# One region of program order for ScalarE over both borders of the output projection; first tiles split one per product and loaded three ahead; the last mixed tile taken from SBUF instead of a reload

## The chip, the core and the metric

The kernel runs on one core of one Trainium2 chip. The metric is the device time of one execution, in microseconds (us); smaller is better. The engines work side by side, each through its own queue in order: TensorE (PE) multiplies matrices into PSUM, VectorE (DVE), ScalarE (ACT) and GpSimd (POOL) do elementwise work, and SyncE (SP) here only issues DMA transfers.

## What is computed

Two residual layers on a sequence of 1024 tokens and 1024 channels, fp32 in and out.

```python
def short_conv_mixer(h, w_in, w_conv, w_out):
    proj = h @ w_in                                   # (1024, 4 * 2048)
    b_gate, c_gate, u, z = jnp.split(proj, 4, axis=-1)
    v = c_gate * u
    vp = jnp.pad(v, ((0, 0), (CONV_K - 1, 0), (0, 0)))
    conv = sum(w_conv[k] * vp[:, k:k + S] for k in range(CONV_K))
    return (b_gate * conv * jax.nn.silu(z)) @ w_out

def reference(x, ...):
    x = x + short_conv_mixer(rms_norm(x, conv_norm[0]), conv_w_in[0], conv_w[0], conv_w_out[0])
    x = x + dilated_attention_mixer(rms_norm(x, attn_norm[0]), attn_w_in[0], ...)
    return x
```

The attention layer projects to three groups of queries, keys and values with 16 heads each and to a gate z, does windowed attention in each group, merges the groups and projects back. The change lies in the first layer and in the step from the first to the second.

## The kernel before, in words

**Operands.** Each fp32 operand of a product is held as two parts: a high part in the TensorE's fp32r type, made by a copy on ScalarE, and a low part, the rest, made by a subtraction on VectorE. A product takes three matmuls for each of four k tiles: high by high, high by low, low by high, so 12 matmuls of 128x512 (`product`, L302 to L310). Weights are loaded by SyncE into `wr` (two buffers) and split into `ws` (eight buffers) by `split_w`: ScalarE at L159, VectorE at L160. The activations stand in blocks `blka` to `blkg` and `xb`, each of four tiles with a high and a low part.

**Strassen.** Most of the projections go in pairs of weights by one level of Strassen's scheme: seven products instead of eight, with mixed weights (POOL at L280 into `sr`, three buffers) and mixed activations (T[1] to T[4]). `strassen` (L321) runs the seven products in the order 1, 2, 4 of the pair before, 6, 5, 3 of the pair before, 7, and pulls the next weight split out of the generator `prepare` after each. p1's result is copied out of its PSUM bank by ScalarE (`copied`, L314), then p6 accumulates into the same bank, then comes another copy, then p7 and p4 accumulate in the same way; so each needs the copy before it.

**Stages.** (1) The opening, 0 to about 79 us: the first channel tile e=0 and half of e=1 by plain products (`products`, `first_products`, `evac`), while x is normalised, its row statistics are taken (`row_stats`, `row_spread`) and the mixed activations are made (`mixed`). (2) NI = 29 input pairs, to about 635 us. The results y go to DRAM (`ydc`), and their mixed tiles are made in `y_mix` and stored too (`ymd`). (3) The output projection, to about 810 us: n = NI by plain products a to h, n = NI + 1 to NI + 3 by Strassen, then `chunk` for the second half of the k range, with `row` finishing x1, storing it, and making the attention's operands from it. (4) The attention's projections in pairs, to about 1595 us, then (5) the attention.

**The two borders.** At the first border, from input pairs to the output projection, the blocks change their contents from x to y: `plan` (L469) puts a load of each tile (L474) and its split (L479, L480) into numbered slots, one slot to each product, counted from the first product of n = NI - 1; the load stands two slots ahead of the split. At the second border, from the output projection to the attention's pairs, `row` (L709), `third`, `fourth` and `lower` (L744 to L759) fill the blocks from x1. `fourth` and `lower` load x1 again from DRAM (`x1_tile`, L698).

**What sets the order.** TensorE runs in program order inside a `manual_schedule`. ScalarE does so inside three regions: the opening, n = NI - 1 to NI + 3 (one region for each n), and the stage of `chunk` with the first two pairs of the attention. Everything else, and all of VectorE, POOL and SyncE before the attention, is put in order by a scheduler that simulates the kernel's timeline, and it may move an instruction from outside a region ahead of it.

## Time and profile before

| | |
|---|---|
| Median of three runs | 1926.6 us (1923.59 to 1931.82) |
| The profiled execution | 1925.76 us; its span is 1923.9 us |
| TensorE matmul, weight loads | 1883.5 us busy (98%), 1542.7 us (80%) |
| VectorE, ScalarE, POOL | 1510.4 us (79%), 881.0 us (46%), 950.5 us (49%) |
| DMA | 264.29 MB moved, mean 137 GB/s |
| Busy time of TensorE in 660 to 812 us | 152.00 of 152.00 us |
| Busy time of TensorE in 846 to 1595 us | 747.92 of 749.00 us |
| Busy time of TensorE in 1595 to 1924 us | 307.38 of 329.00 us, granted clock 0.96 |

The profile is one execution, so its stages are set against its own span. Busy time is the time in which an engine had an instruction in work. A matmul of 128x512 shows as 0.39 us, since its end overlaps the next; two in a row start 0.227 us apart at full clock. In a timeline row the first two numbers are the start and the length, and the bracket behind it tells how long the engine had stood idle and what it waited for.

### The profile page before, as it was taken

To read this page: it belongs to the slowest core of one execution; us is meant where nothing else is said; L and a number is where in the kernel's file an instruction comes from. 1 tells how busy PE (TensorE), PEld (TensorE's weight loads), DVE (VectorE), ACT (ScalarE), POOL (GpSimd) and SP (SyncE) were. 2 spreads that over 40 slices of the span, in tenths; PEclk is the share of its full clock that TensorE was granted. 3 is DMA by queue.
4 is the path that set the end of the run, shared out by engine and by line. 5 is a ranking of instruction groups with operands and counts; after the bars stand their busy time and mean duration, and the time that the engine had idled before them with its cause. 6 is when DMAs were issued, how large, how long until landed. Compare 5 with 4: busy or idle time off the path is not lost. (4 is left out here: it accounts for less than half of the span.)

```text
span 1923.9 us, 30568 instructions
## 1 busy us (share of the span) xinstructions
PE 1883.5 (98%) x10814; PEld 1542.7 (80%) x10814; DVE 1510.4 (79%) x2794; ACT 881.0 (46%) x2039; POOL 950.5 (49%) x894
## 2 busy tenths in 40 slices
PE   8999999999999999999999999999999998999999
PEld 6888888888888788878888888888888886777877
DVE  7966667777766865678988698888888887988886
ACT  6533333333334443443334343434343437878880
POOL 1376676767576442524545554555454552333240
PEclk9999999999999999999999999999999999899999
DMA  6222233332423774323324332433232337897742
GB/s 213 87 81 90 89 110 126 109 121 98 127 93 127 236 250 165 136 77 121 115 83 131 109 113 81 136 109 113 83 123 95 125 127 253 248 301 242 223 139 88
DMA packets 121514, 264.29 MB, mean 137 GB/s; under 512 B 19134, under 2 KB 24478, under 8 KB 121360
## 3 DMA queue, kind: packets, MB, share of 16 engines
q1 hardware_dynamic: 94432, 178.99, 28.9%
q0 software_dynamic: 26928, 83.34, 13.0%
q8 instruction: 85, 1.39, 0.3%
q14 instruction: 69, 0.57, 0.1%
HBM read 194.62 MB, written 76.03 MB: 141 GB/s over the span
## 5 line engine op out<-in xcount | busy, mean ns | idle before, releaser
L280 POOL TENSOR_TENSOR sr<-wr 128x512 f32<-128x512 f32 x144 | 207.6, 1442 | 253.3 <-DMA wr<-in_conv_w_in 113.3
L159 ACT ACTIVATE ws<-sr 128x512 fp32r<-128x512 f32 x288 | 180.3, 629 | 325.6 <-PE pp L309 257.4
L160 DVE TENSOR_TENSOR ws<-sr,ws 128x512 fp32r<-128x512 f32 x288 | 269.4, 942 | 66.3 <-ACT ws L159 64.5
L160 DVE TENSOR_TENSOR ws<-wr,ws 128x512 fp32r<-128x512 f32 x248 | 267.2, 1080 | 63.2 <-ACT ws L159 62.7
L159 ACT ACTIVATE ws<-wr 128x512 fp32r<-128x512 f32 x248 | 154.7, 629 | 288.6 <-PE pp L309 242.9
L318 DVE TENSOR_TENSOR f<-pp,f 128x512 f32<-128x512 f32 x216 | 147.3, 682 | 65.0 <-PE pp L309 57.0
L1085 ACT ACTIVATE xs<-xs,nl 128x256 f32<-128x256 f32 (+2 forms) x384 | 160.7, 427 | 0.0
L314 ACT ACTIVATE f<-pp 128x512 f32<-128x512 f32 x240 | 139.3, 581 | 9.5 <-PE pp L309 9.5
L280 POOL TENSOR_TENSOR sr<-wr,sr 128x512 f32<-128x512 f32 x72 | 95.4, 1324 | 77.9 <-issue 67.4
L306 PE MATMUL pp<-blka,ws 128*128 128x512 f32 x328 | 127.8, 390 | 3.0 <-ACT blka L690 2.3
L308 PE MATMUL pp<-blka,ws 128*128 128x512 f32 x328 | 128.0, 390 | 1.4 <-DVE blka L691 1.4
L306 PE MATMUL pp<-blkb,ws 128*128 128x512 f32 x328 | 128.2, 391 | 0.0
L309 PE MATMUL pp<-blka,ws 128*128 128x512 f32 x328 | 127.8, 390 | 0.0
L309 PE MATMUL pp<-blkb,ws 128*128 128x512 f32 x328 | 127.7, 389 | 0.0
L308 PE MATMUL pp<-blkb,ws 128*128 128x512 f32 x328 | 127.6, 389 | 0.0
L306 PE MATMUL pp<-blkg,ws 128*128 128x512 f32 x320 | 124.7, 390 | 0.0
L309 PE MATMUL pp<-blkg,ws 128*128 128x512 f32 x320 | 124.5, 389 | 0.0
L308 PE MATMUL pp<-blkg,ws 128*128 128x512 f32 x320 | 124.5, 389 | 0.0
L306 PE MATMUL pp<-blkf,ws 128*128 128x512 f32 x296 | 118.1, 399 | 3.2 <-ACT f L314 2.9
L1079 DVE CUSTOM_DVE_ANT_0 xs<-ps,bt 128x256 f32<-128x256 f32 (+2 forms) x384 | 102.5, 325 | 21.3 <-PE pt L1092 13.2
L308 PE MATMUL pp<-blkf,ws 128*128 128x512 f32 x296 | 116.1, 392 | 1.0 <-DVE blkf L480 0.7
L309 PE MATMUL pp<-blkf,ws 128*128 128x512 f32 x296 | 115.9, 392 | 0.0
(321 smaller groups left out, 5022.3 us busy)
## 6 DMA issues: line engine op xcount, KB each, us to landing
wr<-in_conv_w_in SPq DMA_DIRECT2D x128, 256.0 KB, 3.1
wr<-in_wqk SPq DMA_DIRECT2D x96, 256.0 KB, 3.2
qkd<-blkc POOLq DMA_DIRECT2D x48, 512.0 KB, 4.3
qk<-qkd SPq DMA_DIRECT2D x48, 512.0 KB, 5.1
f<-in_x SPq DMA_DIRECT2D x48, 256.0 KB, 5.0
f<-ydc SPq DMA_DIRECT2D x48, 256.0 KB, 4.8
wr<-in_wv SPq DMA_DIRECT2D x48, 256.0 KB, 3.1
vd<-blkc POOLq DMA_DIRECT2D x96, 128.0 KB, 2.8
```

What stands on the lines that cost most here:

```text
L159: nc.scalar.activation(t[:, 0], src, AF.Copy)
L160: nc.vector.tensor_tensor(t[:, 1], src, t[:, 0].bitcast(F32), op=OP.subtract)
L280: nc.gpsimd.tensor_tensor(t, x, y, op=op)
L306: nc.tensor.matmul(ps, w[:, 0, ws], b[:, k, 0], start=new and k == 0, stop=False, skip_group_check=skip)
L308: nc.tensor.matmul(ps, w[:, 0, ws], b[:, k, 1], start=False, stop=False, skip_group_check=skip)
L309: nc.tensor.matmul(ps, w[:, 1, ws], b[:, k, 0], start=False, stop=end and k == 3, skip_group_check=skip)
L314: nc.scalar.activation(t, ps, AF.Copy)
L318: nc.vector.tensor_tensor(m, ps, m, op=OP.add)
L1079: nc.vector.tensor_tensor_reduce(out=x, in0=flat[s][:, cols], in1=u["bt"][s][:, bs], op0=OP.add, op1=OP.min, scale=-1.0, scalar=3e38, accu ...
L1085: nc.scalar.activation(x, x, AF.Exp, bias=nm, scale=-1.0, accum_out=L)
```

## The change

The part of the kernel between the two borders becomes one region of program order for ScalarE (`ordered`), entered at n = NI - 1 of the input pairs and left after the first product of pair n = 2 of the attention. TensorE's region begins at the start of the opening instead of behind it, in one piece. The tiles of y are split at most one per product at first, in a new order of blocks (c behind f), and loaded three slots ahead. In n = NI the plain products b and c are exchanged. The first weights of the attention's pairs are split between the last rows (`first_w`, `begun`) instead of ahead of the pairs. The last mixed tile, `fourth(3)`, takes x1 while it is in SBUF in `row(0, 7)`.

```diff
@@ opening of the pools
-            tc.tile_pool(name="pp", bufs=3, space=PSUM) as pp, ... tc.tile_pool(name="cst", bufs=1, space=PSUM) as cst:
+            tc.tile_pool(name="pp", bufs=3, space=PSUM) as pp, ... tc.tile_pool(name="cst", bufs=1, space=PSUM) as cst, \
+            tc.manual_schedule(engines={mybir.EngineType.PE}):
...
-        def strassen(sources, pair, between, made, after=lambda: iter(()), strict=()):
-            w = [list(prepare(*sources[0]))[-1]]
+        def strassen(sources, pair, between, made, after=lambda: iter(()), strict=None, begun=None):
+            w = [begun or list(prepare(*sources[0]))[-1]]
...
-                with tc.manual_schedule(engines={mybir.EngineType.Activation}) if n in strict else nullcontext():
-                    for at, (name, who) in enumerate(order):
+                if n == strict:
+                    ordered.__enter__()
+                for at, (name, who) in enumerate(order):
...
+        ordered = tc.manual_schedule(engines={mybir.EngineType.Activation})
...
-        with tc.tile_pool(name="rp", bufs=1, side="right") as rp, tc.tile_pool(name="cp", bufs=2, side="right") as cp, \
-                tc.manual_schedule(engines={mybir.EngineType.PE}):
+        with tc.tile_pool(name="rp", bufs=1, side="right") as rp, tc.tile_pool(name="cp", bufs=2, side="right") as cp:
...
-                jobs.setdefault(slots[k - 2], []).append(load)
+                jobs.setdefault(slots[min(k - 3, len(slots) - 1)], []).append(load)
...
-            for i, k in enumerate((1, 1, 2, 2)):
-                plan(k, YB, (0, 0), "a", i, ydc[0, i])
-            for i, k in enumerate((3, 3, 4, 4)):
-                plan(k, YB, (1, 0), "b", i, ydc[0, i + 4])
...
-            for i, k in enumerate((7, 7, 8, 8)):
-                plan(k, YT, 1, "c", i, ymd[1, i])
...
+            for ks, d, key, slot in (((1, 2, 3, 4), YB, (0, 0), "a"), ((5, 5, 6, 7), YB, (1, 0), "b"),
+                                     ((6, 7, 8, 8), YB, (1, 1), "d"), ((9, 9, 10, 10), YB, (0, 1), "f"),
+                                     ((11, 11, 12, 12), YT, 1, "c"), ((13, 13, 14, 14), YT, 2, "g"),
...
-                        (0, 0, 0), (0, 0, 1), (1, 0, 0), (1, 0, 1), (0, 1, 0), (1, 1, 0), (0, 1, 1), (1, 1, 1)))}
+                        (0, 0, 0), (1, 0, 0), (0, 0, 1), (1, 0, 1), (0, 1, 0), (1, 1, 0), (0, 1, 1), (1, 1, 1)))}
...
@@ row(hf, dt)
                     if dt < 4:
                         kept[i] = x1
+                    elif dt == 7:
+                        nc.vector.scalar_tensor_tensor(V1[3], x1, g2[:, dt:dt + 1], V1[3], op0=OP.mult, op1=OP.subtract)
@@ fourth(i)
-                t, kt = x1_tile(0, i + 4), i + 4
-                nc.vector.scalar_tensor_tensor(t, t, g2[:, kt:kt + 1], V1[i], op0=OP.mult, op1=OP.subtract)
+                t, kt = V1[3] if i == 3 else x1_tile(0, i + 4), i + 4
+                if i < 3:
+                    nc.vector.scalar_tensor_tensor(t, t, g2[:, kt:kt + 1], V1[i], op0=OP.mult, op1=OP.subtract)
                 parts_of(T[4], i, t)
...
+            first_w = prepare(*sources(pairs[0]))
...
+                    if i == 3:
+                        for _ in range(1 if (hf, dt) == (0, 7) else 2):
+                            w0 = next(first_w)
...
             def between(n, at):
+                if (n, at) == (2, 0):
+                    ordered.__exit__(None, None, None)
...
-            last = strassen([sources(p) for p in pairs], pair, between, lambda: None, strict=range(2))
+            last = strassen([sources(p) for p in pairs], pair, between, lambda: None, begun=w0)
```

Three places show how the instructions move. Line numbers of the changed kernel differ by one or two up to L372 (L159 is L160 there, L314 is L315, L370 is L372) and by more behind that (L479 is L481, L690 and L693 are L678 and L681, L698 is L686, L713 is L701).

**ScalarE in the opening.** Before, ahead of the copy of R (the inverse row norm, out of PSUM bank `st`), behind the last squares of x: `ws` from one `wr` tile are the two halves of one weight tile; in turn W(0, 3), W(1, 0), W(1, 1) and the weights 1 and 2 of the first Strassen pair.

```order
L159 ACTIVATE ws_381<-wr_378 128x512
L159 ACTIVATE ws_384<-wr_378 128x512
L159 ACTIVATE ws_576<-wr_573 128x512
L159 ACTIVATE ws_579<-wr_573 128x512
L159 ACTIVATE ws_677<-wr_674 128x512
L159 ACTIVATE ws_680<-wr_674 128x512
L159 ACTIVATE ws_770<-wr_764 128x512
L159 ACTIVATE ws_773<-wr_764 128x512
L241 ACTIVATE R_125<-st_437 128x512
L242 ACTIVATE sqacc_83<-R_125 128x512
```

Of the changed kernel, the same engine from the second copy of R on: only `ws_383` and `ws_386` stand ahead of the first copy now, and W(1, 0) stands here, behind SiLU and the two taps of tile e=0.

```order
L242 ACTIVATE R_127<-st_521 128x512
L243 ACTIVATE sqacc_83<-R_127 128x512
L365 ACTIVATE f_531<-f_531 128x512
L372 ACTIVATE g_535<-vb_467,conv_w_68 128x512
L372 ACTIVATE g_567<-vb_467,conv_w_68 128x512
L160 ACTIVATE ws_578<-wr_575 128x512
L160 ACTIVATE ws_581<-wr_575 128x512
```

Further on in the changed kernel, from the taps of e=1 to the copy of p1 of the first Strassen pair: all six weights that are split from the pair's loads and mixes and the last mixed tile of x stand between them.

```order
L372 ACTIVATE g<-vb,conv_w 128x512 x2
L160 ACTIVATE ws<-wr 128x512 x2
L160 ACTIVATE ws<-sr 128x512 x3
L160 ACTIVATE ws<-wr 128x512
L160 ACTIVATE ws<-sr 128x512
L206 ACTIVATE blkf<-f 128x512 x4
L315 ACTIVATE f<-pp 128x512
```

The eight splits have gone from one run ahead of R to their places in the program, each close to the product that uses it.

**ScalarE at the first border.** Before, from the second half of b to p7's copy (L314) of the last input pair: `blkc` is a mixed tile out of `ymd`.

```order
L479 ACTIVATE blkb<-f 128x512 x2
L479 ACTIVATE blkc<-f 128x512 x2
L159 ACTIVATE ws<-wr 128x512
L370 ACTIVATE g<-vb,conv_w 128x512
L479 ACTIVATE blkd<-f 128x512 x2
L314 ACTIVATE f<-pp 128x512
L479 ACTIVATE blkd<-f 128x512 x2
```

The same place in the changed kernel:

```order
L481 ACTIVATE blka<-f 128x512
L372 ACTIVATE g<-vb,conv_w 128x512
L481 ACTIVATE blkb<-f 128x512 x2
L315 ACTIVATE f<-pp 128x512
L481 ACTIVATE blkb<-f 128x512
L481 ACTIVATE blkd<-f 128x512
L481 ACTIVATE blkb<-f 128x512
L481 ACTIVATE blkd<-f 128x512
```

The splits of c and d have moved behind the copy, and c behind f.

**SyncE at the second border.** Before, the loads of x1 for `row` (L713), for `fourth` and `lower` (L698), and the weights of the first three attention pairs:

```order
L713 DMA f<-x1d 128x512 x4
L154 DMA wr<-in_wqk 128x512 x4
L713 DMA f<-x1d 128x512 x3
L154 DMA wr<-in_wqk 128x512 x4
L713 DMA f<-x1d 128x512 x2
L698 DMA f<-x1d 128x512 x3
L154 DMA wr<-in_wv 128x512 x3
L698 DMA f<-x1d 128x512 x2
L154 DMA wr<-in_wv 128x512
L698 DMA f<-x1d 128x512 x3
```

And in the changed kernel:

```order
L701 DMA f<-x1d 128x512 x4
L155 DMA wr<-in_wqk 128x512 x4
L701 DMA f<-x1d 128x512 x4
L155 DMA wr<-in_wqk 128x512
L701 DMA f<-x1d 128x512
L155 DMA wr<-in_wqk 128x512 x3
L686 DMA f<-x1d 128x512 x3
L155 DMA wr<-in_wv 128x512 x4
L686 DMA f<-x1d 128x512 x4
```

The load of row (1, 7), and then that of row (0, 7), have moved ahead of the second pair's weights; one reload of `fourth` is gone, and all four of `lower` stand behind the four weight loads of the third pair, where the first stood ahead of the fourth of them.

## The prediction

> **What bounds the kernel now.** I read the page first, then the busy time stage by stage, then the waits of TensorE, then the timelines of the engines around each of its gaps.

> ```profile
> span 1923.9 us, 30568 instructions
> PE 1883.5 (98%) x10814; PEld 1542.7 (80%) x10814; DVE 1510.4 (79%) x2794; ACT 881.0 (46%) x2039; POOL 950.5 (49%) x894
> ```

> TensorE works for 98% of the span, and its 1925.76 us run is the span and 1.86 us around it. Nothing in the change removes a matmul. So it can only give back time in which TensorE stood or ran slowly, or add such time. Columns of the next view: stretch, its length, then busy time of each engine; behind POOL stand the granted clock of TensorE, the DMA share and GB/s.

> ```profile
> 0.00:80.00 80.00, 71.96 (x316) 58.71 (x317) 66.06 (x113) 48.24 (x79) 15.59 (x22) 1.00 0.54 180
> 80.00:635.00 555.00, 553.16 (x2428) 453.95 (x2426) 396.97 (x434) 209.20 (x362) 366.38 (x301) 1.00 0.33 107
> 635.00:643.00 8.00, 5.11 (x16) 3.85 (x15) 8.00 (x9) 5.17 (x10) 5.05 (x3) 0.79 0.50 167
> 654.00:660.00 6.00, 5.27 (x22) 3.75 (x21) 6.00 (x7) 3.56 (x7) 4.71 (x6) 1.00 0.54 169
> 812.00:818.00 6.00, 5.42 (x23) 3.95 (x22) 4.44 (x7) 2.77 (x5) 3.10 (x3) 1.00 0.35 125
> 834.00:846.00 12.00, 8.25 (x27) 6.27 (x27) 10.14 (x13) 6.04 (x11) 5.02 (x3) 0.72 0.25 82
> ```

> The first border (635 to 643, and an echo at 654) and the second (812 to 846) lose time, and at 0.79 and 0.72 the clock was down too. The 555 us of input pairs lose only 1.8 us: nothing of size is to be had there, but much can be lost. The waits of TensorE between 400 and 900 us name who was late (total, times, longest):

> ```profile
> PE pp L306 <- ACT f L314: 4.7, 3, 2.9
> PE pp L306 <- ACT blka L690: 2.3, 1, 2.3
> PE pp L308 <- DVE blka L691: 1.4, 1, 1.4
> PE pp L308 <- DVE blkf L480: 0.7, 1, 0.7
> ```

> **Border 1, what goes.** The timelines of TensorE, of ScalarE and of POOL:

> ```profile
> 634.85 0.39 PE L309 MATMUL pp<-blka,ws 128*128 128x512 f32 x1
> 638.13 0.50 PE L306 MATMUL pp<-blkf,ws 128*128 128x512 f32 x1 [2.89 <-ACT f L314]
> ...
> 642.83 0.39 PE L308 MATMUL pp<-blkb,ws 128*128 128x512 f32 x1
> ```

> ```profile
> 632.70 0.63 ACT L479 ACTIVATE blkc<-f 128x512 fp32r<-128x512 f32 x1 [3.74 <-DMA f<-ymd]
> 633.85 0.63 ACT L479 ACTIVATE blkc<-f 128x512 fp32r<-128x512 f32 x1 [0.51 <-DMA f<-ymd]
> ...
> 635.84 0.72 ACT L370 ACTIVATE g<-vb,conv_w 128x512 f32<-128x512 f32 x1 [0.84 <-DVE vb L639]
> ...
> 637.51 0.57 ACT L314 ACTIVATE f<-pp 128x512 f32<-128x512 f32 x1
> ```

> ```profile
> 632.08 1.29 POOL L638 TENSOR_TENSOR f<-f,sqacc 128x512 f32<-128x512 f32 x1 [8.57 <-DVE f L318]
> ```

> Matmuls start 0.227 us apart elsewhere (553.16 us for 2428 of them in the input pairs is 0.228 each). The last of tile `a` starts at 634.85, so the next was due at 635.08; it came at 638.13, 3.05 late. It is p4 of the last input pair, and accumulates into the bank that p7's copy (L314) has to read first; ScalarE waited for two DMAs of the mixed tile c (the split hoisted out of the next region), which also kept VectorE from making `vb`. From 638.13 to 642.83 thirteen steps took 4.70 instead of 2.95: 1.75 more, at about half the clock. Together **4.8 us**. In the new order the splits of c come four products later, and ahead of p7's copy stand only splits whose ydc tiles are loaded long before. What is late next is the chain c12 (VectorE), its product with R2 (POOL), `vb`, taps, two b splits, copy: from the end of the last p3 that is 0.68 + 1.29 + 0.68 + 0.72 + 1.1 + 0.57 and handovers, some 5.3 us, against the 5.4 us of the product and the tile in between. A remaining wait of 0 to 1 us, I take 0.3: **−4.5**. The echo at 654 to 660 is a wait for VectorE's L480; f is now split ahead of c and loaded three products ahead: of some 1.3 us lost (6.00 less 5.27, and restarts at 0.33 for 0.23) I take **−1.0** (0 to −1.3).

> **Border 2.** TensorE, ScalarE and the DMA issues of SyncE's queue:

> ```profile
> 836.48 0.50 PE L306 MATMUL pp<-blka,ws 128*128 128x512 f32 x1 [2.30 <-ACT blka L690]
> 838.43 0.80 PE L308 MATMUL pp<-blka,ws 128*128 128x512 f32 x1 [1.45 <-DVE blka L691]
> ...
> 844.40 0.39 PE L308 MATMUL pp<-xb,ws 128*128 128x512 f32 x1
> ```

> ```profile
> 835.18 0.72 ACT L693 ACTIVATE blkb<-f,attn_norm 128x512 fp32r<-128x512 f32 x1 [4.16 <-DMA f<-x1d]
> 835.81 0.61 ACT L690 ACTIVATE blka<-f 128x512 fp32r<-128x512 f32 x1
> ```

> ```profile
> 827.92 1.63 SPq L154 DMA_DIRECT2D wr<-in_wv  x3
> 829.65 0.84 SPq L698 DMA_DIRECT2D f<-x1d  x2
> ```

> The last mixed tile (`fourth(3)`) needs x1 reloaded from DRAM, and that load stands behind three weight loads: issued at 829.65, split at 835.81. Counting steps as above, the two waits cost 2.46 + 1.72 and the slow matmuls to 844.40 about 2.5: **6.7 us**. The change makes that tile in `row(0, 7)` while x1 is still in SBUF: one VectorE operation is moved, a 256 KB DMA falls, so this wait is gone. Its cost in the new place is one L711 (0.75, as L753 today) ahead of blkf's low part, on a VectorE that the 812 to 818 row shows busy for 4.44 of 6 us; there today's waits (6.00 less 5.42, and two restarts, 1.2 us) end because the loads of rows (1, 7) and (0, 7) now stand ahead of the second wqk tile; I take 0.2 left: **−1.0**. What is late next: the four reloads of `lower` now stand behind all four wv loads instead of one of them ahead of the fourth, and their VectorE low parts have `spread`'s transpose (which frees the bank `st`) queued behind them. By today's row a reload issued at 829.65 was split at 835.18; four of them at about 0.7 each end near 839 to 840, and p3 of the first attention pair, two products behind p4, wants them at about 839. So **+2.0** (0, if they land as the first does today, to 4, as the 2.30 and 1.45 above with a fall of the clock). Sum of border 2: −6.7 − 1.0 + 2.0 = **−5.7**; both borders: **−11.2** (−7.5 to −13.5).

> **The opening, where I see the price.** The order of ScalarE moves here too, although no line of the opening changed: the eight weight splits that ran ahead of R are now two, and the others stand at their place in the program.

> ```profile
> 31.75 2.18 ACT L159 ACTIVATE ws<-wr 128x512 fp32r<-128x512 f32 x4
> 37.19 1.28 ACT L159 ACTIVATE ws<-wr 128x512 fp32r<-128x512 f32 x2 [3.26 <-PE pp L391]
> 40.11 0.63 ACT L159 ACTIVATE ws<-wr 128x512 fp32r<-128x512 f32 x1 [1.65 <-DMA wr<-in_conv_w_in]
> 42.60 0.63 ACT L159 ACTIVATE ws<-wr 128x512 fp32r<-128x512 f32 x1 [1.85 <-PE pp L391]
> ...
> 57.72 0.63 ACT L159 ACTIVATE ws<-sr 128x512 fp32r<-128x512 f32 x1
> ```

> ```profile
> 46.53 1.21 DVE L65 TENSOR_TENSOR rtt<-rt 128x4 f32<-128x4 f32 x1
> 59.96 0.68 DVE L160 TENSOR_TENSOR ws<-sr,ws 128x512 fp32r<-128x512 f32 x1
> 76.79 0.67 DVE L412 TENSOR_TENSOR vb<-pp,f 128x512 f32<-128x512 f32 x1
> 77.53 0.71 ACT L370 ACTIVATE g<-vb,conv_w 128x512 f32<-128x512 f32 x1
> ```

> ```profile
> 57.52 0.39 PE L389 MATMUL pp<-blka,ws 128*128 128x512 f32 x1
> 79.28 0.39 PE L306 MATMUL pp<-blka,ws 128*128 128x512 f32 x1
> PE st L240 <- DVE rt L67: 1.2, 1, 1.2
> ```

> First a gain: POOL's weight mixes no longer stretch the small VectorE operations of the second row statistic (1.21 at 46.53 us), so TensorE's 1.2 us wait for rt goes: −1.2. Then four waits:
> - W(1, 0), today at 57.52 without a wait. Its splits now follow the taps, in the place of the one at 57.72, so the high half comes at 58.35 and the low half, whose place on VectorE is that at 59.96, at 60.6. The third matmul, due 0.45 after the first, waits some 2.7; with the 1.2 gained the chain itself starts earlier as well: +2.4.
> - W(1, 1): its low halves stand behind L410 of the product that has only just ended: L410, a low part of blke, ws, three times 0.68, less 0.45: +1.7.
> - p1 of the first pair, at 79.28 today: splits behind the second taps, which wait for `vb` of the product that just ended: 0.67 + 0.71 + 0.63 and two handovers to the high half, 0.3 more to the low one: +2.5.
> - p6 of that pair: p1's copy now stands behind six splits, one of which needs a POOL mix whose buffer comes free late, and four of blkf. Eleven operations at 0.545 (x4 in 2.18) are 6.0 us against the 5.4 of two products; with the mix (some 1.3, as POOL's row at 632.08) and handovers: +2.2.

> Sum −1.2 + 8.8 = **+7.6**. The lower end is 3, if the queues ahead run dry earlier than my replay says; the upper 15, if they bring down the clock as at 638.13. Does an idle TensorE slow there? 2.89 us of waiting did it, 2.30 and 1.45 close together did it, while this one, without a slow matmul behind it, did not:

> ```profile
> 1596.64 3.43 PE L1064 MATMUL ps<-qk 64*64 64x128 f32 x48 [2.04 <-DVE ps L994]
> ```

> My four waits lie at and above 2.04 and below 2.89, each some 11 us from the next but the last two; I leave the clock out of the sum and put it among the rivals, at 3 in 10. [...]

> **Input pairs, and the rest.** In the pairs with z, SiLU now comes ahead of the taps and of a split, and it waits for POOL's product with R; the copy that p7's bank waits for stands behind it. The first row of the waits has 4.7 − 2.9 = 1.8 us in two such places today. I count four new ones of 0.6 to 1.1 and two old ones gone (1.3): **+1.5** (−1.3 to 3.5). The spread-out splits of a, and loads three ahead, cost nothing while TensorE runs through these pairs (553.16 of 555 us); without that cover a split is 0.63. The swap of (0, 0, 1) and (1, 0, 0) only gives blkb one product, 2.7 us, more. The attention is in the same order on every engine.

> **Sum.** −11.2 + 7.6 + 1.5 = −2.1 on 1925.76, that is 1923.7; the median of the three runs, 1926.6, lies 0.84 above the profiled one, so I say **1924.5**: no change that can be told, since a measurement of this kernel tells about 0.5%, 9.6 us, from no change.

> **Rivals.**
> - The opening hides its splits (a net of −1 to +1): for it, VectorE and ScalarE together have free time there (66.06 and 48.24 of 80 us). Against it, three of the four splits wait for a product that has just ended, which no free time mends. Then 1926.6 − 11.2 and about +1: 1916. Chance 0.18.
> - Slower: the clock falls in the opening. Each fall costs 1.75 (638.13) to 2.5 us (838.43), and a slow spell at each of the four waits is about +8.5: 1933; with the upper ends of the waits 1937. It decides from the point where the opening takes more than the 11.2 less 1.5 that the rest brings. For it: 2.30 and 1.45 us together sufficed. Against: 2.04 did not. Chance 0.17.
> - The border change doesn't do what it says: p7's copy stays late since c12 goes through POOL and VectorE just ahead of it. If 3 us remain at border 1 and 4 at border 2, −11.2 becomes −5.5: about 1930. Chance 0.10.
> - The forecast: 0.55, by itself 1919 to 1930.

> Range 1914 to 1935: it takes in the hidden opening and the third rival, and leaves out the upper end of the slow clock. Faster by over 0.5% (below 1917) 0.18; slower by over 0.5% (above 1936.2) 0.10; within it 0.72.

> **What would show it.** Right: no wait of p4 for the copy near 638 and none for blka near 836, a clock of 1.00 in both stretches, and 635 to 846 shorter by 9 to 13 us; in 0 to 100 us a TensorE busy share that is lower, with waits for ws and vb at W(1, 0), W(1, 1), p1 and for the copy at p6. Wrong: an opening no longer than now, slow matmuls at 0.43 us between 55 and 95 us, or a new wait for blkb or for `st` at about 840 us of over 4 us.

## The result, and the profile after

The changed kernel takes 1943.55 us (median of six runs, 1937.88 to 1945.26) against 1928.32 us for the kernel before (six runs, 1923.59 to 1934.17). The ratio is 1.0078 with a 95% interval of 1.0060 to 1.0095: slower by 0.8%, some 15 us. The prediction said 1924.5 in a range of 1914 to 1935, and gave slower by over 0.5% a chance of 0.10. It was wrong.

The profiled run of the changed kernel took 1945.26 us, its span 1943.5, so 19.6 us more than the profiled span before. The account below is made between these two traces. That it is 19.6 here and 15 between medians comes from the place of the two profiled runs: 1925.76 lies below five of the six runs of before, and 1945.26 is the highest of its six.

TensorE executes almost the same matmuls in the same order in both, so the clearest account is the start of the same matmul in both traces, and how the difference grows:

| matmul | before | after | difference | grown by | forecast for this step |
|---|---|---|---|---|---|
| p1 of the first pair | 79.28 | 86.56 | +7.3 | | |
| p5 of the first pair | 87.44 | 99.92 | +12.5 | +12.5 | +7.6 |
| p7 of the input pair at 553 us | 553.45 | 572.89 | +19.4 | +7.0 | +1.5 |
| last p3 of the input pairs | 645.35 | 660.22 | +14.9 | −4.6 | −4.5 |
| product on blkd behind the blkf products | 660.25 | 680.24 | +20.0 | +5.1 | −1.0 |
| p6 (xb) of the first attention pair | 816.42 | 835.30 | +18.9 | −1.1 | −1.0 |
| first transposes of rtok in `spread` | 848.04 | 867.95 | +19.9 | +1.0 | −4.7 |
| end of the span | 1923.9 | 1943.5 | +19.6 | −0.3 | 0 |

The waits of TensorE in the changed kernel, in 0 to 100 us, 100 to 635 us, and 635 to 900 us (total, times, longest). Line numbers are those of the changed kernel. In the first stretch TensorE also waited 6.7 us for the very first weights (6.1 before) and 0.7 us for R (0.8 before):

```profile
PE pp L307 <- ACT f L315: 2.8, 1, 2.8
PE pp L393 <- DVE ws L161: 2.2, 2, 1.2
PE pp L307 <- ACT ws L160: 2.1, 1, 2.1
PE pp L391 <- ACT ws L160: 1.3, 2, 0.7
```

```profile
PE pp L307 <- ACT f L315: 6.0, 9, 1.4
```

```profile
PE st L104 <- DVE f L110: 4.8, 1, 4.8
PE pp L309 <- DVE blkf L482: 1.6, 2, 0.9
PE pp L307 <- ACT blkf L481: 1.2, 1, 1.2
```

The first four are the opening's four waits that the prediction named, in the places it named. The next is the input pairs: nine waits of p7 for the copy, where the kernel before had two with 1.8 us. In the last three the long waits of before are gone (the copy at the first border, blka at the second), and two others stand there: blkf at 671 us and the bank st at 862 us. TensorE's timeline at three of these places (start, length, and in the bracket the wait):

```profile
57.13 0.50 PE L391 MATMUL pp<-blka,ws 128*128 128x512 f32 x1 [0.62 <-ACT ws L160]
57.46 0.40 PE L392 MATMUL pp<-blka,ws 128*128 128x512 f32 x1
58.87 0.78 PE L393 MATMUL pp<-blka,ws 128*128 128x512 f32 x1 [1.01 <-DVE ws L161]
59.45 0.63 PE L391 MATMUL pp<-blka,ws 128*128 128x512 f32 x1
```

```profile
671.08 0.50 PE L307 MATMUL pp<-blkf,ws 128*128 128x512 f32 x1 [1.18 <-ACT blkf L481]
672.46 0.50 PE L309 MATMUL pp<-blkf,ws 128*128 128x512 f32 x1 [0.88 <-DVE blkf L482]
...
674.16 0.80 PE L309 MATMUL pp<-blkf,ws 128*128 128x512 f32 x1 [0.74 <-DVE blkf L482]
674.75 0.63 PE L310 MATMUL pp<-blkf,ws 128*128 128x512 f32 x1
```

```profile
861.96 1.12 PE L104 MATMUL st<-ident,ms 128*128 128x128 f32 x4 [4.79 <-DVE f L110]
862.73 0.78 PE L307 MATMUL pp<-blkd,ws 128*128 128x512 f32 x1
863.30 0.63 PE L309 MATMUL pp<-blkd,ws 128*128 128x512 f32 x1
```

A length of 0.63 instead of 0.39 us is a matmul at half clock: the granted clock there is 0.50. Behind each of these three places, and behind p6's wait at 95.47 us, matmuls then start 0.427 us apart, at a granted clock of 0.50 for 3.41 us (from 58.92 and 96.47 us) or 6.83 us (from 673.32 and 861.06 us); that adds 1.7 to 2.9 us each time.

What TensorE waits for at 671 us is seen on ScalarE:

```profile
659.68 0.62 ACT L160 ACTIVATE ws<-sr 128x512 fp32r<-128x512 f32 x1
669.87 0.63 ACT L365 ACTIVATE f<-f 128x512 f32<-128x512 f32 x1 [9.57 <-POOL f L631]
670.41 1.14 ACT L481 ACTIVATE blkf<-f 128x512 fp32r<-128x512 f32 x2
```

The second half of blkf's splits stands behind the last SiLU (L365), which waits 9.57 us for POOL's product of c12 with R. At 862 us it is a load. SyncE's queue, then ScalarE:

```profile
848.00 2.11 SPq L155 DMA_DIRECT2D wr<-in_wv  x4
850.15 10.24 SPq L686 DMA_DIRECT2D f<-x1d  x4
```

```profile
855.44 0.72 ACT L681 ACTIVATE blkb<-f,attn_norm 128x512 fp32r<-128x512 f32 x1 [3.30 <-DMA f<-x1d]
```

The four reloads of `lower` go out behind all four weight loads of the third pair; ScalarE and then VectorE wait for the first of them, and the transpose that frees st (L110) stands on VectorE behind its low part and four more operations, from 856.20 to 861.20 us.

### The profile page after: what moved, and what is told of

Its sections match the earlier page's. It is cut to its first block, busy times and chain, and to the rows that moved or that the text cites. A ratio compares the mean times of both kernels' runs of the same rounds, so it can differ in the third digit from the quotient of the medians.

```text
span 1943.5 us, 30568 instructions
## 1 busy us (share of the span) xinstructions
PE 1888.3 (97%) x10814; PEld 1542.3 (79%) x10814; DVE 1483.0 (76%) x2794; ACT 873.7 (45%) x2039; POOL 938.6 (48%) x894
## 3 DMA queue, kind: packets, MB, share of 16 engines
q8 instruction: 85, 1.39, 0.3%
## 5 line engine op out<-in xcount | busy, mean ns | idle before, releaser
L161 DVE TENSOR_TENSOR ws<-wr,ws 128x512 fp32r<-128x512 f32 x248 | 262.4, 1061 | 94.0 <-ACT ws L160 93.7
L161 DVE TENSOR_TENSOR ws<-sr,ws 128x512 fp32r<-128x512 f32 x288 | 264.6, 924 | 81.3 <-ACT ws L160 80.1
L160 ACT ACTIVATE ws<-sr 128x512 fp32r<-128x512 f32 x288 | 179.2, 628 | 326.0 <-PE pp L310 239.6
L160 ACT ACTIVATE ws<-wr 128x512 fp32r<-128x512 f32 x248 | 154.0, 626 | 220.5 <-PE pp L310 197.8
L315 ACT ACTIVATE f<-pp 128x512 f32<-128x512 f32 x240 | 139.4, 581 | 9.0 <-PE pp L310 9.0
L309 PE MATMUL pp<-blka,ws 128*128 128x512 f32 x328 | 127.6, 389 | 0.0
L309 PE MATMUL pp<-blkb,ws 128*128 128x512 f32 x328 | 127.6, 389 | 0.0
L309 PE MATMUL pp<-blkg,ws 128*128 128x512 f32 x320 | 124.5, 389 | 0.0
L307 PE MATMUL pp<-blkf,ws 128*128 128x512 f32 x296 | 118.9, 402 | 1.2 <-ACT blkf L481 1.2
L307 PE MATMUL pp<-blke,ws 128*128 128x512 f32 x288 | 113.4, 394 | 6.2 <-ACT f L315 6.0
L309 PE MATMUL pp<-blkf,ws 128*128 128x512 f32 x296 | 116.7, 394 | 1.6 <-DVE blkf L482 1.6
```

The costliest lines, as they stand in the source:

```text
L160: nc.scalar.activation(t[:, 0], src, AF.Copy)
L161: nc.vector.tensor_tensor(t[:, 1], src, t[:, 0].bitcast(F32), op=OP.subtract)
L307: nc.tensor.matmul(ps, w[:, 0, ws], b[:, k, 0], start=new and k == 0, stop=False, skip_group_check=skip)
L309: nc.tensor.matmul(ps, w[:, 0, ws], b[:, k, 1], start=False, stop=False, skip_group_check=skip)
L315: nc.scalar.activation(t, ps, AF.Copy)
```

## The experiments

The theory to test (R): the region does not begin at n = NI - 1 but where its object is made. `ordered = tc.manual_schedule(...)` stands ahead of the opening, and only `__enter__` stands at n = NI - 1. ScalarE's order in the opening and in every input pair is then the program's, not the scheduler's, and the first 19.4 us of the table are the price. The rival (T) was that the loads three ahead and the new table of splits make the waits of the pairs. For the two borders, the question was which edit made the new waits. Eleven kernels ran, in three groups on one chip each, with the kernel before beside them. "Difference" is again that of the same matmul against the trace of before. Each trace is one execution: in e3 and e4, whose edits lie behind the input pairs, the difference still changes by −2.0 and +2.0 us between the first pair's p5 and 553 us, so 2 us in the pairs, whether they come from the scheduler or from the run, are no finding. One more thing stays out of the question. TensorE stands in program order through the opening in the kernel before, too (its first region begins at L351, ahead of it); the change only makes one region of two, and e1 keeps that.

### e1: the region begun where it is entered

```diff
-        ordered = tc.manual_schedule(engines={mybir.EngineType.Activation})
+        ordered = []
...
                 if n == strict:
-                    ordered.__enter__()
+                    ordered.append(tc.manual_schedule(engines={mybir.EngineType.Activation}))
+                    ordered[0].__enter__()
...
-                    ordered.__exit__(None, None, None)
+                    ordered[0].__exit__(None, None, None)
```

> The changed kernel, with one edit: the object of ScalarE's region is made at n = NI - 1, where it is entered, and no longer ahead of the opening. Theory R: the region holds from the line where its object is made, so ScalarE stands in program order through the opening and all input pairs, and that alone costs the +12.5 us that the traces show up to the first pair's p5 and the +7.0 us of the input pairs. R expects both gone: the first matmul of the last p4 on blkf at 634 to 635 us (654.7 in the changed kernel, 638.1 before), and a time some 19 us below the changed kernel, near 1926, within 3 us of the kernel before. Rival T: the loads three ahead and the table of splits make the waits of the input pairs; then at least the 7 us stay and the time is 1931 or more. Both expect the waits at blkf (about 671 - 19 us) and at st (862 - 19 us) to stay.

Measured: 1924.56 us against 1926.62 for before, ratio 0.9993 (0.9974 to 1.0013), so 2.1 us below the kernel before, where the changed kernel was 15.2 above the one beside it; between the traces the gain is 19.0 us. The first matmul of p4 on blkf starts at 634.57 us; at 515 us the difference is −0.3, where the changed kernel had +18.9. TensorE's waits in 100 to 635 us are one row:

```profile
PE pp L307 <- ACT f L315: 1.0, 1, 1.0
```

R stands and T falls: with the table, the loads, the reload and the attention's first weights all as in the change, the opening and the pairs run as before. The waits at blkf and st stayed (5.2 us at st).

### e2: the region alone, on the kernel before

```diff
+        ordered = tc.manual_schedule(engines={mybir.EngineType.Activation})
...
-                with tc.manual_schedule(engines={mybir.EngineType.Activation}) if n in strict else nullcontext():
+                if n == strict:
+                    ordered.__enter__()
...
-            with tc.manual_schedule(engines={mybir.EngineType.Activation}):
-                chunk(0, 0, 0)
+            chunk(0, 0, 0)
...
+                if (n, at) == (2, 0):
+                    ordered.__exit__(None, None, None)
```

> The kernel before, with ScalarE's single region alone, made ahead of the opening as in the change (TensorE's region in one piece, since regions have to nest); old table of splits, loads two ahead, reload kept. R: the opening and the input pairs lose 19.4 us as in the changed kernel; the wait of p4 for the copy (4.8 us at 638) goes, since no split can be moved out of the next product any more; the reload's 6.7 us at 836 stay. So 1926 + 19.4 - 4.8, about 1941. T: the opening and pairs run as before, about 1922.

Measured: 1954.08 us, ratio 1.0147 (1.0126 to 1.0167). The difference is +14.3 at p7 of the first pair and +19.3 at 553 us: the region alone makes the loss of the opening and the pairs. In 100 to 635 us:

```profile
PE pp L307 <- ACT f L315: 6.0, 7, 1.6
```

It is 13 us more than R said, since another 9.1 us are lost between 660 and 848 us, nearly all at the second border, where program order puts the first attention weights behind the last row (the change had moved them between the rows). The first border gained only 3.1 us where the changed kernel gained 4.6 (p4 still waits 1.2 us for the copy), and the wait at blkf came (+4.3) with the old table: it belongs to the region, not to the table.

### e3: the table, the loads and the exchange alone

```diff
-                jobs.setdefault(slots[k - 2], []).append(load)
+                jobs.setdefault(slots[min(k - 3, len(slots) - 1)], []).append(load)
...
+            for ks, d, key, slot in (((1, 2, 3, 4), YB, (0, 0), "a"), ((5, 5, 6, 7), YB, (1, 0), "b"),
...
-                        (0, 0, 0), (0, 0, 1), (1, 0, 0), (1, 0, 1), (0, 1, 0), (1, 1, 0), (0, 1, 1), (1, 1, 1)))}
+                        (0, 0, 0), (1, 0, 0), (0, 0, 1), (1, 0, 1), (0, 1, 0), (1, 1, 0), (0, 1, 1), (1, 1, 1)))}
```

> The kernel before, with the new table of splits, loads three ahead and the exchange of two plain products alone; regions as before. Expected by the traces: border 1's 4.8 us go (the c splits stand four products later), the wait for blkf behind SiLU grows by 5.1 us net if the table causes it (theory S1: splits of b, d and f moved later pile up on VectorE ahead of the last c12), so within 2 us of before, 1925 to 1928. If the single region causes it (S2), only the gain is left: 1921 to 1922.

Measured: 1928.18 us, ratio 1.0016 (0.9999 to 1.0032). Neither theory had it right. The waits in 635 to 900 us begin with

```profile
PE pp L306 <- ACT f L314: 6.2, 2, 5.9
```

so p4 still waits for the copy, 5.9 us instead of 2.9: with a region for each n, the scheduler moves other splits of the next region ahead of the copy, three of d at 628.9 to 631.5 us. What they delay is on VectorE: two of their low parts and one of a weight stand ahead of `vb`, and `vb` (634.12 us) and the two operations just ahead of it took 1.75 to 1.79 us each while POOL worked, for 0.68 us otherwise; the taps and p7's copy wait for `vb`. Only the region keeps these splits behind the copy. The wait at blkf is gone here (from 638 to 660 us the difference falls from +0.1 to −1.5). That fits what e2 says: where the first border's wait is kept, VectorE and POOL have the time to finish c12, and blkf is not late; where it is removed, TensorE arrives 4.6 us earlier and meets the same chain.

### e4: the reload of the last mixed tile left out, alone

```diff
+                    elif dt == 7:
+                        nc.vector.scalar_tensor_tensor(V1[3], x1, g2[:, dt:dt + 1], V1[3], op0=OP.mult, op1=OP.subtract)
...
-                t, kt = x1_tile(0, i + 4), i + 4
+                t, kt = V1[3] if i == 3 else x1_tile(0, i + 4), i + 4
```

> The kernel before, with the last mixed tile made in the row while x1 is in SBUF, and nothing else. Theory L1: p4's waits (6.7 us) go, but the loads of the lower tiles then stand behind the weights and TensorE waits about 5 us for the bank st and loses about 2.5 us to half clock: within 2 us of before. L2: the new wait comes from the early split of the first attention weights in the same change; then alone this edit gains about 6.7 us: 1919 to 1920.

Measured: 1924.11 us, ratio 0.9998 (0.9983 to 1.0013). In 635 to 900 us blka is no longer waited for, and st is:

```profile
PE st L104 <- DVE f L110: 3.2, 1, 3.2
```

L1 stands for the wait, and L2 falls: it comes with this edit alone. The granted clock stayed at 1.00 here from 800 to 880 us, so from 816 to 848 us the trace is 3.5 us shorter, but the runs don't tell it from no change.

### e5: the reloads of the lower tiles issued earlier (on e1)

```diff
-                parts_of(B[1, 1], i, x1_tile(1, i + 4), g2[:, i + 4:i + 5])
+                parts_of(B[1, 1], i, low.pop(i) if i in low else x1_tile(1, i + 4), g2[:, i + 4:i + 5])
+
+            low = {}
+
+            def fetch_low(i):
+                low[i] = x1_tile(1, i + 4)
...
+            for k, i in ((4, 0), (5, 1), (6, 2), (6, 3)):
+                rest.setdefault(k, []).append((fetch_low, i))
```

> e1 (region made where it is entered) and the four reloads of the lower tiles issued in the first attention pair, two ahead of all weights of the third pair and two ahead of the last of them, instead of behind them. Theory D: TensorE waits 5.2 us for the bank st and then runs at half clock because VectorE's low parts of blkb wait for these loads; then the wait falls below 1 us, the clock stays at 1.00, and the time is 6 to 8 us below e1: 1917 to 1919. Rival B: VectorE's backlog is what st waits for; then 3 us or more of the wait stay and the time is within 3 us of e1.

Measured: 1919.46 us against 1924.81, ratio 0.9968 (0.9949 to 0.9988); e1's was 0.9993. The clock stays at 1.00 from 800 to 880 us, and the wait is

```profile
PE st L104 <- DVE f L110: 1.5, 1, 1.5
```

From 816 to 848 us the trace gains 5.6 us on e1's; between the ratios it is 4.8 us, and their intervals overlap, so the trace has to carry it. D stands for the most part: of the 5.2 us that st waited, 3.7 belong to the loads behind the weights, though 1.5 us are left where D said under 1.

### e6: the splits of f ahead of SiLU (on e1)

```diff
-                                     ((6, 7, 8, 8), YB, (1, 1), "d"), ((9, 9, 10, 10), YB, (0, 1), "f"),
+                                     ((6, 7, 8, 8), YB, (1, 1), "d"), ((9, 9, 9, 9), YB, (0, 1), "f"),
```

> e1 and all four splits of f in the slot of the product ahead of the last p3 (9, 9, 9, 9 for 9, 9, 10, 10), so that on ScalarE they stand ahead of the SiLU that waits for POOL's product of c12 with R. Theory Q: the 4 us lost at blkf at 650 us (1.2 for ScalarE, 1.6 for VectorE and a slow clock behind) come from the order on ScalarE alone, where the second half of f stands behind SiLU; then they go, and the time is 4 to 6 us below e1, 1919 to 1921. Rival V: VectorE is full from the border on, and whatever stands later waits instead; then the sum from 630 to 680 us stays within 1.5 us of e1's.

Measured: 1921.05 us, ratio 0.9980 (0.9967 to 0.9993). From 553 us to the start of the product on blkd the trace gains 5.2 us on e1's, and in 600 to 900 us blkf is not waited for at all:

```profile
PE st L104 <- DVE f L110: 5.1, 1, 5.1
PE pp L307 <- ACT f L315: 0.6, 1, 0.6
```

Q stands, V falls: VectorE was busy for 38.02 of 40 us from 640 to 680, and TensorE waits for none of its results there. The place of two splits behind SiLU on ScalarE was the whole cause of this wait, and with it out of the way the trace keeps the first border's gain. The runs are below the kernel before by 0.2%, but their interval overlaps that of e1.

### e7: e5 and e6 together

> e5 and e6 in one kernel. D and Q: the two gains lie 150 us apart and add, 10 to 13 us below e1, 1912 to 1915, and 0.6 to 0.7% below the kernel before, a ratio of 0.993 to 0.994. B and V: no more than 4 us below e1, a ratio of 0.997 or more.

Measured: 1916.08 us, ratio 0.9954 (0.9936 to 0.9972). The gains that the runs of e5 and e6 showed over e1, 0.25% and 0.13%, add: 0.9993 less both is 0.9955. Against the 10 to 13 us that were expected from the traces a part is missing, and the profiled run, the slowest of the six (1921.93 us), shows one place: at 666 us p6 of the output projection's first Strassen pair waits for a copy that stands behind splits of e, and those wait for loads. With the slow matmuls behind it 4.2 us are lost there.

```profile
666.65 0.56 PE L307 MATMUL pp<-blkg,ws 128*128 128x512 f32 x1 [2.03 <-ACT f L315]
667.00 0.63 PE L309 MATMUL pp<-blkg,ws 128*128 128x512 f32 x1
```

### e8: the region begun where it is entered, alone, on the kernel before

e2's edit, with the object made as in e1.

> The kernel before with one region for ScalarE from n = NI - 1 on, its object made where it is entered; old table of splits, loads two ahead, reload and order of the first attention weights as before. R: the opening and the input pairs as before (offset within 1 us at 600 us), where e2, the same region made ahead of the opening, is 19 us late by then: 1926 to 1936, at least 18 us below e2. Of the rest, some 10 us that e2 lost between 800 and 850 us (the first attention weights split behind the last row) should be here too, if they belong to program order at the second border. T: more than 5 us late by 600 us.

Measured: 1933.00 us, ratio 1.0040 (1.0023 to 1.0057), 21 us below e2. The difference is −2.9 at 515 us: R again. From 660 to 816 us 6.0 us are lost, by the wait

```profile
PE pp L307 <- ACT ws L160: 2.9, 1, 2.9
```

and slow matmuls behind it, which have no more than the other 3.1 us: the first attention weights stand behind the last row, as in e2. In e1, which has the change's split of these weights between the rows, nothing is lost from 660 to 812 us; so the region needs that split once it spans the second border, as far as one can tell without taking the new table out as well.

### e9: the mixed tiles e and f later (on e7)

```diff
-                                     ((15, 15, 16, 16), YT, 3, "e"), ((17, 18, 20, 21), YT, 4, "f"),
+                                     ((17, 18, 19, 20), YT, 3, "e"), ((21, 22, 23, 24), YT, 4, "f"),
```

> e7 and the mixed tiles e and f split later (17, 18, 19, 20 and 21, 22, 23, 24 for 15, 15, 16, 16 and 17, 18, 20, 21), so that the copy of the first Strassen product of the output projection no longer stands on ScalarE behind splits of e that wait for their loads. Theory W: the 2.2 us wait and the slow clock behind it that e7's trace shows at 666 us go (3.9 us there, 0.8 in e6), and the time is 1 to 4 us below e7: a ratio to before of 0.993 to 0.995. Rival: the loads themselves are late (f buffers are short), p7 then waits for blke in place of the copy, and the time stays within 1 us of e7.

Measured: 1915.72 us against 1924.76, ratio 0.9948 (0.9930 to 0.9967). In the trace the wait at 666 us and the slow clock behind it are gone (granted clock 1.00 from 640 to 680 us, 0.96 in e7). But p7 of the same pair now waits for its copy, which stands behind a split that waits 4.55 us for a weight mix of POOL:

```profile
672.52 0.50 PE L307 MATMUL pp<-blke,ws 128*128 128x512 f32 x1 [1.40 <-ACT f L315]
```

So 1.9 us are lost there in place of 4.2, and the clock falls at 820.68 us, where it did not in e7 (0.96 and 1.00 from 800 to 840 us). The medians differ by 0.4 us, where W said 1 to 4: W is right about the wait that goes and not about the time, and the rival has the time but not its reason, for p7 waits for the copy and not for blke. This kernel has the lowest ratio of the study, within e7's interval: faster than before by 0.5%, and than the changed kernel by about 1.3% (0.9948 by 1.0078).

### e10: SiLU behind the copy in the input pairs (on the changed kernel)

```diff
-                        gate_z(e, 0, c11)
+                        v["c11"] = c11

                 def p6():
                     product(v["x"], w[6], T[2], False, True)
                     v["u2"] = copied(v["x"])
+                    if pr:
+                        gate_z(e, 0, v["c11"])
```

> The changed kernel, with SiLU of the first z half recorded behind the copy of p6's bank instead of ahead of it, in every input pair with z; nothing else. Theory Z: the 7.0 us of the input pairs are p7's waits for that copy, which stands behind a SiLU that waits for POOL; then the offset against before no longer grows from 120 to 600 us (1 us at most, for 7.0), and the time is 5 to 7 us below the changed kernel. Rival: the copy then waits for the taps of vb instead, and at least 4 of the 7 us stay. Both expect the opening's 12.5 us to stay.

Measured: 1940.35 us, ratio 1.0076 (1.0050 to 1.0102). The waits in 100 to 635 us went from 6.0 to

```profile
PE pp L307 <- ACT f L315: 4.9, 8, 1.4
```

and the difference grew from +13.9 at p7 of the first pair to +17.3 at 526 us, by 3.5 instead of 7.0. Neither theory is settled by this. The ratio is the changed kernel's (1.0078) within its interval, and e11 below, which leaves SiLU where it is, grows by 3.1 us in the same stretch. What the trace does show is which waits are left. One of 1.4 us, at 104 us, is the first pair's. Three of p7 (1.9 us, where the changed kernel had nine with 6.0) stand behind taps (g from vb) that wait 5.9 to 7.0 us for VectorE's `vb`; the other four (1.7 us) are new: p4 waits for p7's copy, behind the taps of the second half. So the copies do wait for the taps once SiLU is out of the way, as the rival says.

### e11: two weights of the opening split early (on the changed kernel)

```diff
+                early = [raw_split(1, k) for k in range(2)]
                 row_spread(0)
                 row_stats(1)
...
             for k in range(2):
-                plain_w(1, k, 2)
+                W[k] = early[k]
                 next(mix)
```

with `raw_split` making the same load and the same two splits as `plain_w`.

> The changed kernel, with the splits of W(1, 0) and W(1, 1) recorded ahead of the copy of R, where the kernel before had them, and nothing else; the first Strassen pair's weights stay behind the taps. Theory R2: program order costs by the place of these splits; the first two of the opening's four waits go, with the fall of the clock behind the first: the offset against before at p1 of the first pair (79.3 us before, +7.3 in the changed kernel) is +0.5 to +2.5, and the two later waits stay, with p6's 2.9 us. In all 5 to 6.5 us below the changed kernel. Rival: the waits come from VectorE's backlog behind the mixed tiles, and less than 2 us are gained.

Measured: 1936.96 us, ratio 1.0057 (1.0035 to 1.0079). The difference at p1 of the first pair is +2.5 (changed kernel: +7.3), and two waits are left in 0 to 100 us beside the first of all and two small ones:

```profile
PE pp L307 <- ACT ws L160: 2.8, 1, 2.8
PE pp L307 <- ACT f L315: 2.8, 1, 2.8
```

R2 stands: the first two waits of the opening are the place of these four splits on ScalarE, and the other two stay. The opening costs 7.7 instead of 12.5 us in the trace; between the ratios the gain is 4 us, with intervals that overlap.

## Why the prediction was wrong, point by point

The steps that failed are four terms: the opening, the input pairs, the echo at blkf, and the wait for st. They were too small by 4.9, 5.5, 6.1 and 5.7 us; the first border and the wait for blka came as said.

**The opening (+7.6 said, +12.5 measured).** The mechanism and all four places were right. Taken apart at the same matmuls: the wait for rt went (−1.2 said, −1.2 measured); W(1, 0) cost 2.1 in two waits, one for each half of the weight (+2.4 said); W(1, 1) 2.4 (+1.7); p1 2.8 (+2.5); p6 2.9 (+2.2). That is 9.0 us where the sum had 7.6. The other 3.5 us are the fall of the clock behind W(1, 0), 1.7, and behind p6, 1.7. The prediction left this out of the sum as a rival with a chance of 3 in 10 (0.17 in its list), because it read a rule out of two rows: that 2.04 us were not enough and 2.89 were. The traces show no such limit (below), and one of its own four terms, 1.7, lay under it. This step failed in size.

**The input pairs (+1.5 said, +7.0 measured).** The prediction saw that ScalarE's order had changed "although no line of the opening changed", and priced it where it looked, without asking what had moved it. e1, e2 and e8 show what: the region reaches back to where its object is made, so all 29 pairs stand in program order. It did name the z pairs' SiLU, which waits for POOL ahead of the copy that p7's bank waits for, as it stands here:

```profile
491.73 0.63 ACT L365 ACTIVATE f<-f 128x512 f32<-128x512 f32 x1 [8.75 <-POOL f L600]
...
493.92 0.58 ACT L315 ACTIVATE f<-pp 128x512 f32<-128x512 f32 x1
```

But it counted four new waits and two gone, and there were nine with 6.0 us. Six of them (4.3 us) are in z pairs, with SiLU, the taps and two splits ahead of the copy. The other three (1.7 us) are in the pairs between, which it did not look at: there the copy stands behind a split that waits 6.0 to 7.6 us for a weight mix of POOL. How much falls to each instruction is open (e10), and so is the size itself: with the same order in the pairs it was 7.0 us here and 3.1 in e11. These 555 us had only 1.8 us to win, and the prediction said so itself; a change that touches the order there can hardly gain.

**Border 1 (−4.5 said, −4.6 measured).** Right in size and in what held the copy: p4 follows p7's tile without a wait, and the granted clock is 1.00 from 600 to 669 us. But the prediction put it down to the splits of c standing four products later. e3 and e2 show that it takes the region: with the new table alone the wait was 5.9 us, with the region alone c's splits stand behind the copy and 1.2 us of the wait are left, and with both none.

**The echo at blkf (−1.0 said, +5.1 measured).** Wrong in sign. The prediction took it for a question of where f's splits stand against c's. What holds them is SiLU in front, which waits for the chain c12, POOL; that chain didn't become faster, and TensorE now arrived 4.6 us earlier than the border's wait had let it. A wait of 1.3 us and 4.6 us of earlier arrival are 5.9; 1.3 + 5.1 = 6.4 us was measured, with the fall of the clock in it (0.70 from 669 to 680 us). So the first border's gain was handed back 15 us later. e6, which moves two splits ahead of that SiLU, keeps it (5.2 us on e1).

**Border 2 (−4.7 said for the reload and what follows it, +1.0 measured; for rows (1, 7) and (0, 7) −1.0 said, −1.1 measured).** p4's wait for blka went, as said, and the new wait stands where it was said, for st behind the reloads of `lower`. Its size was +2.0 in the sum and came to 7.7: a wait of 4.8 us and 2.9 us for the slow matmuls behind it. The sum had taken today's 5.5 us from a reload's issue to its split for all of them; in the change the weight loads ahead waited in SyncE's queue until 848.00, so the first reload was issued only at 850.15 and split at 855.44, and VectorE's queue then took 5.8 us more to reach L110. e5 shows that it is the loads for the most part: issued earlier, 1.5 us of the wait are left.

**The rivals.** The result is the second (slower by a falling clock in the opening) in its place, but by its time (1933 to 1937) it is short by what the pairs and the echo cost. No rival had the region reaching over the pairs. Two of the signs that the prediction gave for being wrong came: slow matmuls between 55 and 95 us, and a wait for st of over 4 us.

## What to carry to other kernels

Where a diff moves instructions at a place that it doesn't mention, find out what moved them before pricing the move: here that one question tells that 550 us of schedule were given up, and the object that opens a region must be made where the region is to begin. A wait that is removed in a chain of tight places is a gain only if what TensorE meets next is ready that much earlier: look for the next instruction that waits for another engine, and for what stands behind it in its queue. In such a place the order of two splits against one SiLU, or of four loads against four others, is worth as much in the trace as the whole first repair (5.2 and 5.6 us against 4.6), and both together, with the region begun where it is entered, make the change a gain (e7: 0.9954, 0.9936 to 0.9972).

## What the runs showed of the hardware that was not expected

In these traces the clock of TensorE did not fall by the length of one wait. In the changed kernel waits of 0.62 and 1.01 us, 1.4 us apart, brought matmuls to 0.427 us apart (59 us), and so did one of 2.03 us in e7 (666 us); yet 2.11 us at 86.56 us in the changed kernel did not, and neither did 3.18 us in e4:

```profile
844.35 0.65 PE L104 MATMUL st<-ident,ms 128*128 128x128 f32 x4 [3.18 <-DVE f L110]
844.76 0.48 PE L306 MATMUL pp<-blkd,ws 128*128 128x512 f32 x1
845.08 0.40 PE L308 MATMUL pp<-blkd,ws 128*128 128x512 f32 x1
```

| kernel | window, us | TensorE busy in it, us | granted clock in the next window |
|---|---|---|---|
| changed | 55.51 to 58.92 | 1.77 | 0.50 |
| e7 | 663.53 to 666.95 | 1.39 | 0.50 |
| changed | 82.82 to 86.23 | 1.63 | 1.00 |
| changed | 86.23 to 89.65 | 2.95 | 1.00 |
| e4 | 839.38 to 842.80 | 1.79 | 1.00 |
| e4 | 842.80 to 846.21 | 1.86 | 1.00 |

The edge of a window cuts the 3.18 us of e4 in two. Over all thirteen traces, from 20 to 900 us, the clock fell behind each of the 25 windows at full clock with less than 1.48 us of busy time (1.25 and 0.74 us in the kernel before; 1.00, 1.36 and 0.00 us in the changed kernel), behind 3 of the 8 with 1.48 to 1.77, and behind only three others. In those (e2, e9, e10) TensorE was busy for 3.0 to 3.2 us, but one entry of 1.84 us in each is sixteen matmuls of a single column (L91). Whether the clock fell for that, no run shows.

For a sum on this kernel these windows give an estimate: waits of about 2 us within 3.41 us carry a chance of 1.7 us more (one window at half clock) to 2.9 us more (two), which depends on where the grid falls, and waits of less than 1.6 us in all did not bring it down but for the three windows named.
